# First group of a Mamba-2 layer: the second half of the copies of the turned xs, and their multiplication by the step sizes, stand ahead of the next group's first SiLU step

## The chip, the cores and the metric

The program runs on one NeuronCore of a Trainium2 chip. Four engines compute side by side, each through its own queue in order: TensorE (PE, matrix products; its weight loads are PEld), VectorE (DVE), ScalarE (ACT) and GpSimd (POOL). SyncE (SP) issues most transfers from HBM. An instruction starts when its queue has reached it and the semaphores that it waits for are set. The metric is device time in microseconds (us), lower is better.

## The reference

Two layers on a sequence of 256 tokens with 2048 features: a Mamba-2 (SSD) mixer, then sliding-window attention. The change touches the first. Cut to what matters:

```python
zxbcdt = x @ w_in                                   # z | xs, B, C | dt
xbc = silu(conv4(xbc) + conv_b)                     # causal, depthwise
dt = softplus(dt_raw + dt_bias);  a = -exp(a_log)
x_c = xs * dt[..., None]                            # xs times step sizes
cb = einsum("bcqgn,bcsgn->bgcqs", c_c, b_c)
y_diag = einsum("bgcqs,bgrcqs,bcsgrp->bcqgrp", cb, decay_in, x_c)
y = y_diag + y_off + xs * d_skip
y = y * silu(z);  y = rmsnorm_by_group(y) * norm_w
h = y @ w_out                                       # 8 groups of 8 heads of 64
x = layernorm(alpha * x + h)
```

In the kernel one decay matrix over both chunks of 128 tokens takes the place of the states, so that y is a product of `x_c` with (C B) times decay.

## The kernel before

The projection runs in eight groups of ten blocks: B, C, four blocks of xs, four of z, 128 features each. Block 10*g + b is block b of group g; group 0 takes its blocks in another order (z first, one z last). A block is 48 products of 128x128 by 128x256 on PE (`narrow`, L252): each weight and each x is split into a rounded part and a rest (wh, wl; xH, xL), and three products stand for one. The weights come as two halves of 128x1024 into `wr`; ACT rounds each (wh, L164), DVE subtracts to get the rest (wl, L167). There are four buffers of wh and wl, six halves of wr, and four PSUM buffers `mm`, used in turn by blocks and by output units: a product into a buffer that was used four before waits until DVE has read that one.

After a block of B, C or xs, ACT and DVE make the convolution and SiLU (`conv_silu`): ACT L492, three steps on DVE L494, tanh on ACT L497, one product on DVE L498. z has L582 and L583.

Once the xs of a group are there, `turn_xs` (L604) turns them on DVE in blocks of 32x32 into zx, `carry_xs` (L613) copies them on ACT in 16 pieces (four for each j) into xd, and `scale_xs` (L618) multiplies xd by the step sizes in one DVE operation of 128x1024. Then `ymm` multiplies xd by the decays on PE (L631, "the y products"), DVE multiplies by the rest of the decay and adds the skip term (yz, L636 and L642), `gate` multiplies by z and sums squares on POOL (L647, L649, L653) and splits y for the next product on ACT and DVE (yH L661, yL L662). `norm` sums over features on PE (L671), which needs the last sum of squares from POOL. Output units (`out_unit`, L323 to L325) multiply y by w_out, two PSUM tiles each (token half 0 and 1), and DVE adds each to the residual with the group's scale (L332). The first output unit of group 0 stands behind block 16, the second behind block 17.

The order of the work comes from two places. `plan` holds, for each block number, the steps that are called behind that block's SiLU; `between` holds steps that are called ahead of its SiLU, right after its products. The tile framework then orders the calls on each engine by its own priorities and estimates; operations marked with `keep_in_program_order` stay in the order of the calls. `scale_xs` of group 0 is marked (pinned), the copies are not. In group 0 the y products are planned behind block 13.

The lines that set group 0's steps are

```python
at(xs_at, turn_xs, g)                      # xs_at = 9 in group 0
for n, js in enumerate(((0,), (1,), (2, 3)) if g < 2 else ((0, 1), (2, 3))):
    at(xs_at + n, carry_xs, g, js)         # behind blocks 9, 10, 11
at(xs_at + 2 + (g == 0), scale_xs, g)      # behind block 12 in group 0
at(t + pos["y"], ymm, g)                   # behind block 13 in group 0
```

## Time and profile before

| what | value |
|---|---|
| median of 3 runs | 988.09 us (988.04 to 989.66) |
| the profiled execution's own time | 990.41 us |
| its span, first to last instruction | 988.6 us |
| mean granted TensorE clock over the span | 0.995 of full speed |
| PE busy | 975.7 us, 99% of the span |
| DVE busy | 781.8 us, 79% |
| ACT busy | 662.7 us, 67% |
| POOL busy | 103.8 us, 10% |
| moved by DMA | 198.89 MB, 201 GB/s on average |

Busy times are sums of an engine's instructions. The matrix engine is nearly always busy, so the time is close to its sum of products; what can be won or lost is in the few places in which it stands still or runs at a lower clock. Those are read from the waits of PE, from the timeline of single instructions around them and from the granted clock in short windows. A timeline row gives the start in us, the duration of all of its xN instructions together, engine, line, operation, output<-input, and in brackets how long the engine stood idle before and what it waited for.

### The profile page before, as it was taken

How to read it: one execution, taken by the hardware profiler on the slowest of the kernel's cores; microseconds unless marked ns; L12 is line 12 of the kernel's file. 1: busy time of each engine (PE TensorE's matmuls, PEld its weight loads, DVE VectorE, ACT ScalarE, POOL GpSimd, SP SyncE). 2: the span in 40 equal slices, each digit the busy share in tenths (PEclk: the TensorE clock that was granted, in tenths of full speed). 3: DMA queues.
4: the chain of work that ended last, by engine and by line, in shares of the span. 5: the costliest groups of instructions: out<-in, count | busy, mean ns of one | idle time of the engine just before them, and what ended most of it. 6: DMA issues, size and time to landing. Idle time of an engine off the chain costs nothing.

```text
span 988.6 us, 18074 instructions
## 1 busy us (share of the span) xinstructions
PE 975.7 (99%) x7004; PEld 885.2 (90%) x7004; DVE 781.8 (79%) x1202; ACT 662.7 (67%) x1236; POOL 103.8 (10%) x137
## 2 busy tenths in 40 slices
PE   9997999999999999999999999999999999999998
PEld 8996999999998999999999999888898978978976
DVE  7888797886888696787688687989867678766786
ACT  7596786675677667667667567467367777764772
POOL 0000403004002100300300300402100000000003
PEclk9998999999999999999999999999999999999999
DMA  9698477557657656657665664657654646464542
GB/s 357 241 300 291 139 224 231 191 183 224 204 179 249 209 180 216 204 176 230 189 202 180 204 208 137 206 185 263 229 171 157 196 150 201 152 211 149 192 150 86
DMA packets 61557, 198.89 MB, mean 201 GB/s; under 512 B 6848, under 2 KB 11360, under 8 KB 61216
## 3 DMA queue, kind: packets, MB, share of 16 engines
q1 hardware_dynamic: 58528, 188.53, 58.4%
q0 software_dynamic: 2336, 8.69, 2.7%
q8 instruction: 55, 0.90, 0.4%
q10 hardware_dynamic: 608, 0.52, 0.2%
q14 instruction: 30, 0.25, 0.1%
HBM read 195.49 MB, written 2.23 MB: 200 GB/s over the span
## 4 chain that ended last, share of the span: by engine, by line
PE 93%; ACT 3%; DMA 2%; DVE 1%; issue 1%; DVEq 0%; ACTq 0%
PE mm L252 49%; PE mm L979 11%; PE mm L323 9%; PE mm L324 9%; PE mm L325 9%; PE ax L631 2%; ACT wh L164 1%; DMA rb<-rscr 1%; ACT xd L613 1%; PE ax L1119 1%; ACT e L549 1%; DMA wr<-in_wa 0%; PE ax L1112 0%; DVE wl L167 0%; PE mm L390 0%
## 5 line engine op out<-in xcount | busy, mean ns | idle before, releaser
L167 DVE TENSOR_TENSOR wl<-wr,wh 128x1024 fp32r<-128x1024 f32 (+2 forms) x338 | 392.3, 1179 | 92.3 <-ACT wh L164 90.3
L164 ACT ACTIVATE wh<-wr 128x1024 fp32r<-128x1024 f32 (+2 forms) x338 | 331.9, 1010 | 94.3 <-PE mm L252 34.3
L252 PE MATMUL mm<-xH,wh 128*128 128x256 f32 x1280 | 354.8, 277 | 0.0
L252 PE MATMUL mm<-xH,wl 128*128 128x256 f32 x1280 | 354.0, 277 | 0.1
L252 PE MATMUL mm<-xL,wh 128*128 128x256 f32 x1280 | 354.1, 277 | 0.0
L252 PEld LDWEIGHTS mm<-xH,wh 128*128 128x128 f32 x1280 | 240.6, 188 | 1.7 <-ACT wh L198 0.5
L252 PEld LDWEIGHTS mm<-xL,wh 128*128 128x128 f32 x1280 | 240.6, 188 | 1.3 <-issue 0.3
L252 PEld LDWEIGHTS mm<-xH,wl 128*128 128x128 f32 x1280 | 240.4, 188 | 0.3 <-DVE wl L167 0.3
L323 PE MATMUL mm<-wh,yH 128*128 128x512 f32 x256 | 101.2, 395 | 0.0
L324 PE MATMUL mm<-wh,yL 128*128 128x512 f32 x256 | 99.8, 390 | 0.0
L325 PE MATMUL mm<-wl,yH 128*128 128x512 f32 x256 | 99.7, 389 | 0.0
L647 POOL TENSOR_TENSOR yz<-yz,z 128x256 f32<-128x256 f32 x32 | 33.1, 1044 | 473.7 <-DVE yz L642 444.4
L494 DVE SCALAR_TENSOR_TENSOR cv<-mm,pc,cv 128x255 f32<-128x255 f32 x144 | 68.5, 476 | 5.8 <-ACT cv L492 4.5
L252 PE MATMUL mm<-x1H,wh 128*128 128x256 f32 x256 | 71.9, 281 | 0.0
L252 PE MATMUL mm<-x1L,wh 128*128 128x256 f32 x256 | 71.1, 278 | 0.0
L252 PE MATMUL mm<-x1H,wl 128*128 128x256 f32 x256 | 71.0, 278 | 0.0
L979 PE MATMUL mm<-wh,x1H 128*128 128x512 f32 x160 | 63.1, 394 | 0.0
L979 PE MATMUL mm<-wl,x1H 128*128 128x512 f32 x160 | 61.8, 389 | 0.0
L979 PE MATMUL mm<-wh,x1L 128*128 128x512 f32 x160 | 60.9, 390 | 0.0
L497 ACT ACTIVATE xs<-cv 128x256 f32<-128x256 f32 x32 | 13.3, 416 | 69.7 <-DVE cv L494 69.7
L323 PEld LDWEIGHTS mm<-wh,yH 128*128 128x128 f32 x256 | 48.1, 188 | 10.3 <-DVE z L583 1.0
L325 PEld LDWEIGHTS mm<-wl,yH 128*128 128x128 f32 x256 | 48.1, 188 | 10.2
(228 smaller groups left out, 1459.8 us busy)
## 6 DMA issues: line engine op xcount, KB each, us to landing
wr<-in_wa SPq DMA_DIRECT2D x154, 512.0 KB, 5.2
wr<-in_wo SPq DMA_DIRECT2D x64, 512.0 KB, 4.6
wr<-in_wq SPq DMA_DIRECT2D x32, 512.0 KB, 4.6
wr<-in_wg SPq DMA_DIRECT2D x31, 512.0 KB, 5.2
wr<-in_wb SPq DMA_DIRECT2D x16, 512.0 KB, 4.6
wr<-in_wb SPq DMA_DIRECT2D x32, 256.0 KB, 3.9
rb<-rscr SPq DMA_DIRECT2D x11, 512.0 KB, 4.4
wr<-in_wkv SPq DMA_DIRECT2D x8, 512.0 KB, 5.2
```

Source lines behind the costliest of these rows:

```text
L164: m = nc.scalar.activation(h[:, sl], v, AF.Copy)
L167: m = nc.vector.tensor_tensor(l[:, sl], v, h[:, sl].bitcast(F32), ALU.subtract)
L252: m = nc.tensor.matmul(ps, a, b, start=first and i == 0, stop=last and i == 2)
L323: pinned(nc.tensor.matmul(ps, aH[:, k, hs], u.h[:, ks], start=k == 0 and add is None, stop=False), pin)
L324: pinned(nc.tensor.matmul(ps, aL[:, k, hs], u.h[:, ks], start=False, stop=False), pin)
L325: pinned(nc.tensor.matmul(ps, aH[:, k, hs], u.l[:, ks], start=False, stop=k == 3), pin)
L494: nc.vector.scalar_tensor_tensor(a[:, sft:], ps[:, : S - sft], w(3 - sft), a[:, sft:], ALU.mult, ALU.add)
L497: nc.scalar.activation(dst, a[:], AF.Tanh)
L549: m = nc.scalar.activation(e[:, h, cols], rb[:, h, c * P :], AF.Relu, scale=-1.0, bias=rtk[:, c, h0 + h : h0 + h + 1])
L631: nc.tensor.matmul(ps[64 * r : 64 * r + 64, cols], st.xd[:, c, i, 64 * r : 64 * r + 64], e[:, 256:] if c else e[:, :256], start=c == 0, st ...
L647: nc.gpsimd.tensor_tensor(v, v, st.z[i][:], ALU.mult)
L979: m = nc.tensor.matmul(ps[:], (x1H, x1L, x1H)[i][:, kk, hs], (u.h, u.h, u.l)[i][:, ks], start=(kk, i) == (0, 0), stop=ui == 3 and (k, i) = ...
```

## The change

```diff
-        for n, js in enumerate(((0,), (1,), (2, 3)) if g < 2 else ((0, 1), (2, 3))):
-            at(xs_at + n, carry_xs, g, js)
-        at(xs_at + 2 + (g == 0), scale_xs, g)
+        if g == 0:
+            at(9, carry_xs, 0, (0,))
+            between[10] = [(carry_xs, 0, (1,))]
+            between[11] = [(carry_xs, 0, (2, 3)), (scale_xs, 0)]
+        else:
+            for n, js in enumerate(((0,), (1,), (2, 3)) if g < 2 else ((0, 1), (2, 3))):
+                at(xs_at + n, carry_xs, g, js)
+            at(xs_at + 2, scale_xs, g)
```

The copies of j = 1 are called ahead of block 10's SiLU, those of j = 2 and 3 and the multiplication ahead of block 11's. The other groups are as before. On ACT the 16 copies keep their places. On DVE the multiplication moves. In the rows below xd_1023 is the tile of the turned xs of group 0, cv a SiLU's convolution sums (cv_1088 in one, cv_1092 in the other, of block 10), and wl_1180 or wl_1181 the rests of block 14's weights.

DVE, around the SiLU of block 10, before:

```order
L494 TENSOR_SCALAR cv_1088<-mm_1038,pc,cv_1088 128x253
L167 TENSOR_TENSOR wl_1180<-wr_1181,wh_1179 128x1024
L498 TENSOR_SCALAR bt_1087<-bt_1087,cv_1088 128x256
L167 TENSOR_TENSOR wl_1180<-wr_1183,wh_1179 128x1024
L167 TENSOR_TENSOR wl_1249<-wr_1250,wh_1248 128x1024
```

and now:

```order
L494 TENSOR_SCALAR cv_1092<-mm_1038,pc,cv_1092 128x253
L618 TENSOR_TENSOR xd_1023<-xd_1023,dtx 128x1024
L498 TENSOR_SCALAR bt_1091<-bt_1091,cv_1092 128x256
L167 TENSOR_TENSOR wl_1181<-wr_1182,wh_1180 128x1024
L167 TENSOR_TENSOR wl_1181<-wr_1184,wh_1180 128x1024
L167 TENSOR_TENSOR wl_1249<-wr_1250,wh_1248 128x1024
```

The multiplication (L618) has come in right behind block 10's third convolution step, ahead of both halves of wl for block 14. Its old place was 15 operations further on.

PE, at the y products of group 0 (ax_1317 and ax_1329), before (mm_1382 is block 14):

```order
L252 MATMUL mm_1382<-xH,wl_1180 128x256
L252 MATMUL mm_1382<-xH,wh_1179 128x256
L631 MATMUL ax_1317<-e_726,xd_1023 64x256 x2
L631 MATMUL ax_1317<-e_726,xd_1023 64x128 x2
```

and now (mm_1258 is block 13):

```order
L252 MATMUL mm_1258<-xL,wh_1104 128x256
L252 MATMUL mm_1258<-xH,wl_1105 128x256
L631 MATMUL ax_1317<-e_726,xd_1023 64x256 x2
L631 MATMUL ax_1317<-e_726,xd_1023 64x128 x2
```

The y products stood behind the first ten products of block 14 and now stand ahead of all 48 of them, right behind block 13.

DVE, behind the SiLU of block 12, before (wl_1446: the rests for the first output unit; cv_1308: block 13; yz, yH, yL: group 0's y):

```order
L618 TENSOR_TENSOR xd_1023<-xd_1023,dtx 128x1024
L167 TENSOR_TENSOR wl_1446<-wr_1447,wh_1445 128x1024
L494 TENSOR_SCALAR cv_1308<-mm_1258,pc,cv_1308 128x255
L167 TENSOR_TENSOR wl_1446<-wr_1449,wh_1445 128x1024
L494 TENSOR_SCALAR cv_1308<-mm_1258,pc,cv_1308 128x254
L636 TENSOR_TENSOR yz_1316<-ax_1317,el_942 128x512
L494 TENSOR_SCALAR cv_1308<-mm_1258,pc,cv_1308 128x253
```

and now, a little further on in the same stretch:

```order
L642 TENSOR_SCALAR yz_1316<-xs_790,pc,yz_1316 128x256
L636 TENSOR_TENSOR yz_1316<-ax_1329,el_942 128x512
L498 TENSOR_SCALAR xs_1307<-xs_1307,cv_1308 128x256
L642 TENSOR_SCALAR yz_1316<-xs_861,pc,yz_1316 128x256
L642 TENSOR_SCALAR yz_1316<-xs_934,pc,yz_1316 128x256
L662 TENSOR_SCALAR yL_1350<-yz_1316,pc,yH_1349 128x256
L167 TENSOR_TENSOR wl_1446<-wr_1449,wh_1445 128x1024
L662 TENSOR_SCALAR yL_1350<-yz_1316,pc,yH_1349 128x256 x3
```

The second half of wl_1446 has gone from between the convolution steps of block 13 to behind the first yL. ACT and POOL each have one swap of neighbours there (the first yH ahead of a tanh, a transfer issued ahead of an addition).

## The prediction

> **What bounds the kernel now.** I read the page first, then what PE waited for.

> ```profile
> span 988.6 us, 18074 instructions
> PE 975.7 (99%) x7004; PEld 885.2 (90%) x7004; DVE 781.8 (79%) x1202; ACT 662.7 (67%) x1236; POOL 103.8 (10%) x137
> PE 93%; ACT 3%; DMA 2%; DVE 1%; issue 1%; DVEq 0%; ACTq 0%
> ...
> PE ax L631 <- DVE xd L618: 7.1, 1, 7.1
> PE ax L372 <- DVE zero L360: 1.0, 1, 1.0
> ```

> PE is busy for 99% of the span and makes up 93% of the chain that ended last. It waits for another engine twice: 1.0 us at the start, and once for 7.1 us, at the y products (L631), for the multiplication that the change moves. So I read the timeline around that wait, engine by engine, and then the pieces of the chain there and at the same steps later.

> ```profile
> 79.26 2.06 ACT L613 COPY xd<-zx 32x256 f32<-32x256 f32 x5
> 79.27 1.52 DVE L494 SCALAR_TENSOR_TENSOR cv<-mm,pc,cv 128x255 f32<-128x255 f32 x3 [0.43 <-ACT cv L492]
> 82.44 1.22 DVE L167 TENSOR_TENSOR wl<-wr,wh 128x1024 fp32r<-128x1024 f32 x1 [1.66 <-ACT wh L164]
> 87.56 0.28 PE L252 MATMUL mm<-xH,wh 128*128 128x256 f32 x1
> 88.61 0.28 PE L252 MATMUL mm<-xH,wh 128*128 128x256 f32 x1
> 94.40 0.42 DVE L498 SCALAR_TENSOR_TENSOR xs<-xs,cv 128x256 f32<-128x256 f32 x1 [0.54 <-ACT xs L497]
> 94.74 1.22 DVE L618 TENSOR_TENSOR xd<-xd,dtx 128x1024 f32<-128x1024 f32 x1
> ```

> ```profile
> 96.02 5.39 PE ax L631 x32
> 101.41 15.40 PE mm L252 x134
> 123.36 5.47 PE mm L252 x48
> 150.67 2.75 PE ax L631 x32
> ```

> The last copy into xd ends at 79.26 + 2.06 = 81.3. The multiplication runs at 94.74, 13 us later, though it needs nothing else: it stood in its place in DVE's queue. PE ended its ten early products of block 14 (87.56 to 88.61, the first and the last of them) at 88.9 and stood until 96.0. Group 1's y products take 2.75, these took 5.39. The clock says why:

> ```profile
> 88.00:89.00 1.00, 0.89 (x8) 0.69 (x6) 0.68 (x2) 0.19 (x1) 0.00 (x0) 1.00 0.68 254
> 91.00:92.00 1.00, 0.00 (x0) 0.00 (x0) 1.00 (x3) 0.56 (x1) 0.00 (x0) 0.56 0.88 311
> 96.00:97.00 1.00, 0.98 (x6) 0.61 (x8) 1.00 (x1) 0.71 (x1) 0.00 (x0) 0.50 0.77 315
> 101.00:102.00 1.00, 1.00 (x9) 0.67 (x7) 0.67 (x2) 1.00 (x3) 0.92 (x2) 0.82 0.77 307
> ```

> The granted clock is the third number from the end. It is 0.56 in 91 to 92, so it fell to one half at about 91.1 (0.12 of that us at full speed), 2.2 us after PE stopped. It is 0.82 in 101 to 102, so it came back at about 101.4, 5.3 us after PE resumed.

> **The change, part by part.** *The multiplication on DVE.* In its new place DVE has finished the convolution steps at 80.8, the copies end at 81.3, and DVE stood idle for 1.66 us ahead of 82.44. It runs there, 81.3 to 82.5, and the y products have xd 5 us before PE asks. Cost: the two wl halves of block 14 behind it end about 0.4 later; block 14 is then used behind the y products only, so they are covered by 2.75. What follows on DVE until 94.4 is about 0.3 late.

> *The wait of PE.* Block 13 ends at 87.56. The y products follow at once, with a warm clock: 87.6 to 90.35. Blocks 14 to 16 of 5.47 each end at 106.8. In before, they end at 101.41 + 15.40 = 116.8 less a few hundredths. PE is ahead by 7.1 (the wait) + 2.64 (5.39 less 2.75) = 9.8 us. That much would be the gain if all else came early too. It doesn't: DVE, ACT and POOL did other work during the wait and are not 9.8 us ahead. These rows tell what is late next.

> ```profile
> 99.92 0.87 DVE L642 SCALAR_TENSOR_TENSOR yz<-xs,pc,yz 128x256 f32<-128x256 f32 x2
> 100.53 1.18 POOL L647 TENSOR_TENSOR yz<-yz,z 128x256 f32<-128x256 f32 x1 [29.34 <-ACT xs L497]
> 102.61 0.96 DVE L642 SCALAR_TENSOR_TENSOR yz<-xs,pc,yz 128x256 f32<-128x256 f32 x1
> 106.57 0.48 DVE L494 SCALAR_TENSOR_TENSOR cv<-mm,pc,cv 128x255 f32<-128x255 f32 x1 [1.37 <-ACT cv L492]
> 106.97 3.50 DVE L662 SCALAR_TENSOR_TENSOR yL<-yz,pc,yH 128x256 fp32r<-128x256 f32 x2
> 109.43 0.74 POOL L653 TENSOR_TENSOR sq<-sq,sq 128x256 f32<-128x256 f32 x1
> 110.79 1.21 DVE L167 TENSOR_TENSOR wl<-wr,wh 128x1024 fp32r<-128x1024 f32 x1
> 116.00 1.52 DVE L494 SCALAR_TENSOR_TENSOR cv<-mm,pc,cv 128x255 f32<-128x255 f32 x3 [2.14 <-ACT cv L492]
> 116.65 0.50 PE L671 MATMUL ax<-cc,sq 128*128 128x1 f32 x4
> 117.67 0.48 PE L323 MATMUL mm<-wh,yH 128*128 128x512 f32 x1
> 127.88 1.37 DVE L332 SCALAR_TENSOR_TENSOR xr<-mm,r,xr 128x512 f32<-128x512 f32 x2
> 128.67 0.39 PE L323 MATMUL mm<-wh,yH 128*128 128x512 f32 x1
> 131.40 0.39 PE L323 MATMUL mm<-wh,yH 128*128 128x512 f32 x1
> ```

> *First new wait, at norm (L671).* It needs POOL's last sum, which ended at 110.2 for a PE that came at 116.65. POOL starts when DVE has made the first yz (99.92 plus one of two operations). DVE reaches that at 98.0: gone from ahead of it are the multiplication (1.2), the second half of wl_1446 (1.1) and a convolution step (0.4), and 0.8 is paid that the next paragraph names. So POOL starts at 98.6 and, with its 9.6 us (100.53 to 110.17), ends at 108.2. PE comes at 106.8: a wait of about 1.5. Behind it are queued the C B product and the first output unit, 109.3 (1.0 after norm, as 117.67 to 116.65).

> *Second and third, for PSUM.* Block 17 writes the buffer of block 15, free when DVE's three steps at 116.00 end (117.5); the second unit's second half (131.40) writes the buffer of the first unit's first half, free when the first of the two additions at 127.88 ends (128.6). In before, that leaves 2.8 us to spare. So the gain that lasts is 2.8 plus what DVE's additions come earlier. From the wl at 110.79 to 127.88 DVE and ACT do the same work in both kernels and wait for PE nowhere, so the question is what the stretch from 94.40 to 110.79 loses. It loses the multiplication (1.2) and the wait for block 14 (1.4, since the block now ends at 95.8). It pays the 0.3 from above and about 0.5 for waiting on ACT's conversion, which the multiplication had hidden, as here at a like place:

> ```profile
> 90.20 1.22 DVE L167 TENSOR_TENSOR wl<-wr,wh 128x1024 fp32r<-128x1024 f32 x1 [0.52 <-ACT wh L164]
> 159.87 1.76 DVE L167 TENSOR_TENSOR wl<-wr,wh 128x1024 fp32r<-128x1024 f32 x1
> ```

> That is 1.8 us earlier. But the second half of wl_1446 and a SiLU product have moved to where POOL is at work, and there DVE is slower: a yz took 0.96 instead of 0.43, a wl 1.76 instead of 1.21, and two yL 3.50. Bounds for the shift: 2.6 earlier (nothing paid) and nothing. I take 1.1, nearer to the slowed rows (1.8 less 0.55 and 0.53 is 0.7), because POOL works through the whole stretch. So the addition ends at 127.5, block 15's buffer is free at 116.4.

> PE then: first unit 109.3, block 17 at 115.0 (5.69 on, as 117.67 to 123.36), waits 1.4 to 116.4, second unit at 121.7, its second half at 124.5, waits 3.0 to 127.5. Gain there 131.4 - 127.5 = 3.9, and 9.8 less 1.5, 1.4 and 3.0 is 3.9 too. Behind that PE is again what all others wait for: the wl of block 18 follows the additions directly on DVE and PE needs it 2.7 later; the gain stays to the end.

> [...]

> *The clock.* A wait of 3.0 is longer than the 2.2 after which the clock fell. No row shows its price at this length: nothing if it holds, 2.64 as in the wait of 7.1. The ends are far apart; the wait is past the point at which the clock fell, so it is nearer to the row of 2.64 than to nothing: I take 1.4. If it falls at norm instead, most of that is taken out of the waits behind. Gain 3.9 - 1.4 = 2.5.

> *DMA and queues.* SP's order is unchanged. One issue waits for the second half of wl_1446, which now ends about 6 us later (near 105 instead of 98.6):

> ```profile
> 97.12 1.85 SPq L155 DMA_DIRECT2D wr<-in_wa  x2
> wr<-in_wa SPq DMA_DIRECT2D x154, 512.0 KB, 5.2
> 124.80 2.95 ACT L164 ACTIVATE wh<-wr 128x1024 fp32r<-128x1024 f32 x3
> ```

> It lands near 111 and ACT reads it at about 124: cover of 13 us, cost nothing. POOL's transfer, one place earlier, is read 40 us later.

> The sum: a span of 988.6 - 2.5 = 986.1; the profiled execution 990.41 - 2.5 = 987.9. That execution is 2.3 above the median of the runs shown, so against the median: 988.09 - 2.5 = **985.6**.

> **The rivals.** *The clock holds* in the third wait: 988.09 - 3.9 = 984.2. For it: the wait is less than half of 7.1. Against it: the fall after 2.2. [...]

> *DVE and POOL exclude each other in full.* POOL's 9.6 less its two issues of about 0.7 is 8.3; DVE has eight operations of 0.42 and a wl of 1.21 there, 4.6. One after another from 98.6 they end at 111.5, and with two convolution steps of 0.4 the wl at 110.79 comes at 112.3, 1.5 late. So do the additions: gain 2.8 - 1.5 = 1.3, less up to 1.4 for the clock: 986.8 to 988.2. For it: the 3.50 of two yL. Against it: the 0.87 of two yz beside POOL's start.

> *Slower.* The same collisions, worse: each of these nine operations takes the 1.75 of the yL at 106.97. From 98.9 that is 15.8; with 0.6 for the yz read from PSUM and 0.8 for two convolution steps the wl comes at 116.1. The additions are 5.3 late, PE's second half 2.5 later than before: 990.6. It decides from 2.8 on, where the spare time is used up. Against it: POOL's work ends long before.

> *Nothing comes back:* 988.09 - 9.8 = 978.3; against it the L653 and L332 rows. *It doesn't do what it says*, PE waiting for something else at L631: 988.1; against it, the wait names L618 alone and group 1's y products wait for nothing.

> **How the numbers follow.** A measurement of this kernel can tell about 0.2%, 2.0 us, from no change. Forecast 985.6: 0.45, its own range 984.7 (clock price 0.5) to 987.0 (shift 0.5, price 1.9). Clock holds, 983.4 to 984.7: 0.25. Full exclusion: 0.15. Nothing comes back: 0.03. No effect: 0.04. Slower: 0.08. Faster by over 2.0, below 986.1: 0.36 of the forecast's, 0.25, 0.03 and 0.01 of exclusion: 0.65. Slower 0.09, the rest same, 0.26. The range 983.3 to 988.0 reaches over the first three and leaves out what lies beyond.

> **What would show it.** L618 at about 81.3 and no wait of L631 for it; the y products 2.75 long near 87.6; a wait of L671 on POOL of 1 to 3 us; waits of L252 and L323 on DVE L494 and L332; a clock under 1.0 near 127 to 132. Wrong: a gain above 6 (no waits), a wait of L631 that stays, or wl of blocks 14 to 18 late.

## The result, and the profile after

The changed kernel takes 985.32 us in the median of eight runs (984.70 to 986.33). The kernel before, in eight runs (the three of the table above among them), takes 988.84 us (986.81 to 991.18). The ratio is 0.9965, with a 95% interval of 0.9954 to 0.9977: faster by 0.35%, about 3.5 us. The forecast was 985.6 from a base of 988.09, that is a gain of 2.5, and the range 983.3 to 988.0 holds the time. The profiled execution has a span of 984.1 us, 4.5 less than before, at a mean granted clock of 0.999.

The page of the changed kernel and its list of what PE waited for (total us, times, longest) answer to the first lines of the prediction:

```profile
PE 973.6 (99%) x7004; PEld 883.8 (90%) x7004; DVE 783.3 (80%) x1202; ACT 662.7 (67%) x1236; POOL 103.2 (10%) x137
...
PE ax L671 <- POOL sq L653: 2.6, 1, 2.6
PE mm L323 <- DVE xr L332: 2.4, 1, 2.4
PE ax L372 <- DVE zero L360: 1.0, 1, 1.0
```

The wait of 7.1 us is gone. Two new ones stand in its place: 2.6 us at the norm, and 2.4 us at the second half of the second output unit. The timeline around them, in the order of time:

```profile
78.73 2.06 ACT L613 COPY xd<-zx 32x256 f32<-32x256 f32 x5
78.74 1.52 DVE L494 SCALAR_TENSOR_TENSOR cv<-mm,pc,cv 128x255 f32<-128x255 f32 x3 [0.44 <-ACT cv L492]
80.83 1.23 DVE L618 TENSOR_TENSOR xd<-xd,dtx 128x1024 f32<-128x1024 f32 x1 [0.57 <-ACT xd L613]
...
87.20 2.82 PE L631 MATMUL ax<-e,xd 128*64 128x256 f32 x32
98.26 0.73 POOL L647 TENSOR_TENSOR yz<-yz,z 128x256 f32<-128x256 f32 x1 [27.61 <-DVE yz L642]
100.65 2.92 DVE L642 SCALAR_TENSOR_TENSOR yz<-xs,pc,yz 128x256 f32<-128x256 f32 x2
103.89 1.75 DVE L167 TENSOR_TENSOR wl<-wr,wh 128x1024 fp32r<-128x1024 f32 x1
104.53 2.34 POOL L649 TENSOR_TENSOR sq<-yz 128x256 f32<-128x256 f32 x2
105.57 2.45 DVE L662 SCALAR_TENSOR_TENSOR yL<-yz,pc,yH 128x256 fp32r<-128x256 f32 x3
107.94 0.99 DVE L494 SCALAR_TENSOR_TENSOR cv<-mm,pc,cv 128x255 f32<-128x255 f32 x2
108.34 0.74 POOL L653 TENSOR_TENSOR sq<-sq,sq 128x256 f32<-128x256 f32 x1
109.13 0.61 PE L671 MATMUL ax<-cc,sq 128*128 128x1 f32 x4 [2.56 <-POOL sq L653]
...
126.06 1.36 DVE L332 SCALAR_TENSOR_TENSOR xr<-mm,r,xr 128x512 f32<-128x512 f32 x2
126.82 0.50 PE L323 MATMUL mm<-wh,yH 128*128 128x512 f32 x1 [2.37 <-DVE xr L332]
```

The multiplication (L618) runs at 80.83 in DVE's idle time, the y products take 2.82 near 87.2, and POOL's last sum ends at 109.08 for a PE that had come at 106.57. The second half of the output unit starts at 126.82, for 131.40 before. Behind it both kernels need the same time: 988.6 - 131.40 = 857.2 and 984.1 - 126.82 = 857.3. So the whole difference between the traces was made by the time at which that row starts.

Not all of it comes from the change. DVE's row at block 10 (the second above), which no moved operation precedes, is at 79.27 before and at 78.74 here, and lies between 76.74 and 78.82 in the experiments. Most of these differences arise far ahead of the operations that were edited: one and the same subtraction on DVE (wl, L167) starts at 51.07 to 53.07 in the ten traces, behind a wait of ACT of 2.6 to 4.9 us for a transfer (rb). What sets that wait was not tested. PE moves less: its y products start between 86.92 and 87.72 wherever they wait for nothing. Below, a DVE time is therefore given as its distance from that row. The additions (L332) are 127.88 - 79.27 = 48.61 behind it before and 126.06 - 78.74 = 47.32 now, 1.3 earlier. Of the 4.6 us at the second half, 0.5 is where that row lies and 4.05 is left.

The chain of work that ended last shows what holds the first group now (start, us, engine and line):

```profile
80.82 1.06 ACT wh L164
...
100.73 2.84 DVE yz L642 x2
...
123.41 0.69 DVE e L597
...
125.04 1.08 DVE zx L604 x3
126.13 0.65 DVE xr L332
```

Before, the chain came through the multiplication to the y products and stayed on PE. Now it stays on DVE and ACT until 126.8. In this execution the granted clock (third number from the end) did not fall in either wait:

```profile
108.00:109.00 1.00, 0.00 (x0) 0.00 (x0) 0.96 (x4) 0.00 (x0) 0.99 (x2) 1.00 0.53 213
...
125.00:126.00 1.00, 0.00 (x0) 0.00 (x0) 1.00 (x4) 0.92 (x1) 0.00 (x0) 1.00 0.66 262
```

### The profile page after: what moved, and what is told of

It reads as the page before. It is cut to its first block, busy times and chain, and to the rows that moved or that the text cites. A ratio compares the mean times of both kernels' runs of the same rounds, so it can differ in the third digit from the quotient of the medians.

```text
span 984.1 us, 18075 instructions
## 1 busy us (share of the span) xinstructions
PE 973.6 (99%) x7004; PEld 883.8 (90%) x7004; DVE 783.3 (80%) x1202; ACT 662.7 (67%) x1236; POOL 103.2 (10%) x137
## 4 chain that ended last, share of the span: by engine, by line
PE 86%; DVE 5%; ACT 4%; DMA 3%; issue 1%; SPq 1%; ACTq 0%; DVEq 0%
PE mm L252 43%; PE mm L984 11%; PE mm L323 9%; PE mm L325 9%; PE mm L324 9%; PE ax L631 2%; DVE wl L167 2%; DMA wr<-in_wa 1%; ACT wh L164 1%; ACT e L549 1%; DMA rb<-rscr 1%; DMA xr<-in_first 1%; ACT xd L613 1%; PE ax L1124 1%; SPq L192 1%
## 5 line engine op out<-in xcount | busy, mean ns | idle before, releaser
L167 DVE TENSOR_TENSOR wl<-wr,wh 128x1024 fp32r<-128x1024 f32 (+2 forms) x338 | 392.8, 1181 | 88.5 <-ACT wh L164 86.6
L164 ACT ACTIVATE wh<-wr 128x1024 fp32r<-128x1024 f32 (+2 forms) x338 | 332.1, 1010 | 92.4 <-PE mm L252 32.7
L252 PE MATMUL mm<-xH,wh 128*128 128x256 f32 x1280 | 355.0, 277 | 0.0
L252 PE MATMUL mm<-xL,wh 128*128 128x256 f32 x1280 | 354.2, 277 | 0.0
L252 PE MATMUL mm<-xH,wl 128*128 128x256 f32 x1280 | 354.0, 277 | 0.0
L252 PEld LDWEIGHTS mm<-xH,wh 128*128 128x128 f32 x1280 | 240.8, 188 | 2.0 <-ACT wh L198 0.3
L252 PEld LDWEIGHTS mm<-xL,wh 128*128 128x128 f32 x1280 | 240.6, 188 | 0.9
L252 PEld LDWEIGHTS mm<-xH,wl 128*128 128x128 f32 x1280 | 240.6, 188 | 0.0
L323 PE MATMUL mm<-wh,yH 128*128 128x512 f32 x256 | 101.3, 396 | 2.4 <-DVE xr L332 2.4
L647 POOL TENSOR_TENSOR yz<-yz,z 128x256 f32<-128x256 f32 x32 | 32.7, 1030 | 469.6 <-DVE yz L642 469.6
L494 DVE SCALAR_TENSOR_TENSOR cv<-mm,pc,cv 128x255 f32<-128x255 f32 x144 | 68.4, 476 | 4.5 <-ACT cv L492 3.1
L252 PE MATMUL mm<-x1H,wh 128*128 128x256 f32 x256 | 71.9, 281 | 0.0
L252 PE MATMUL mm<-x1L,wh 128*128 128x256 f32 x256 | 71.1, 278 | 0.0
L252 PE MATMUL mm<-x1H,wl 128*128 128x256 f32 x256 | 71.1, 278 | 0.0
L323 PEld LDWEIGHTS mm<-wh,yH 128*128 128x128 f32 x256 | 48.1, 188 | 13.0 <-DVE xr L332 2.8
L497 ACT ACTIVATE xs<-cv 128x256 f32<-128x256 f32 x32 | 13.3, 415 | 66.8 <-DVE cv L494 66.8
L325 PEld LDWEIGHTS mm<-wl,yH 128*128 128x128 f32 x256 | 48.1, 188 | 10.2
## 6 DMA issues: line engine op xcount, KB each, us to landing
wr<-in_wa SPq DMA_DIRECT2D x154, 512.0 KB, 5.2
wr<-in_wo SPq DMA_DIRECT2D x64, 512.0 KB, 4.4
wr<-in_wq SPq DMA_DIRECT2D x32, 512.0 KB, 4.5
wr<-in_wg SPq DMA_DIRECT2D x31, 512.0 KB, 5.0
wr<-in_wb SPq DMA_DIRECT2D x16, 512.0 KB, 4.3
rb<-rscr SPq DMA_DIRECT2D x11, 512.0 KB, 4.1
wr<-in_wkv SPq DMA_DIRECT2D x8, 512.0 KB, 4.8
```

Of the source, the lines that this page charges most:

```text
L164: m = nc.scalar.activation(h[:, sl], v, AF.Copy)
L167: m = nc.vector.tensor_tensor(l[:, sl], v, h[:, sl].bitcast(F32), ALU.subtract)
L252: m = nc.tensor.matmul(ps, a, b, start=first and i == 0, stop=last and i == 2)
L323: pinned(nc.tensor.matmul(ps, aH[:, k, hs], u.h[:, ks], start=k == 0 and add is None, stop=False), pin)
L325: pinned(nc.tensor.matmul(ps, aH[:, k, hs], u.l[:, ks], start=False, stop=k == 3), pin)
L494: nc.vector.scalar_tensor_tensor(a[:, sft:], ps[:, : S - sft], w(3 - sft), a[:, sft:], ALU.mult, ALU.add)
```

## The experiments

All start from the changed kernel. The theory: early waits of PE are forgotten, since the second half of the output unit hangs on DVE's additions, and a wait that leaves the granted clock as it is costs only its length. Its rivals stand with each experiment.

**The copies early, the multiplication later.** The multiplication goes behind block 11's SiLU; the copies are called as in the changed kernel.

```diff
-            between[11] = [(carry_xs, 0, (2, 3)), (scale_xs, 0)]
+            between[11] = [(carry_xs, 0, (2, 3))]
+            at(11, scale_xs, 0)
```

> The multiplication stands behind the SiLU of block 11, between its old and its new place; all else is the changed kernel. Theory (the time is set by VectorE's chain of additions, and PE's early waits are given back later): the multiplication ends near 90, PE waits for it about 3 us at the y products, and then the waits at norm (2.6) and at the second output unit (2.4) shrink by about as much in all; the second half of the second output unit starts within 0.8 us of the changed kernel's 126.8, and the time is that of the changed kernel within 1 us (ratio to the kernel before 0.9965 to 0.9975). Rival (each us that PE waits at the y products costs a us): about 3 us slower than the changed kernel, a ratio of 0.999 to 1.000.

Measured: 986.45 us, ratio 0.9963 (0.9950 to 0.9977) to the kernel before, span 982.8 in the profiled execution. Its waits and rows:

```profile
PE mm L323 <- DVE xr L332: 2.5, 1, 2.5
PE ax L631 <- DVE xd L618: 1.7, 1, 1.7
...
77.04 1.52 DVE L494 SCALAR_TENSOR_TENSOR cv<-mm,pc,cv 128x255 f32<-128x255 f32 x3 [0.44 <-ACT cv L492]
87.38 1.22 DVE L618 TENSOR_TENSOR xd<-xd,dtx 128x1024 f32<-128x1024 f32 x1
...
124.64 1.37 DVE L332 SCALAR_TENSOR_TENSOR xr<-mm,r,xr 128x512 f32<-128x512 f32 x2
```

PE waits 1.7 us for the multiplication again, and the wait at the norm has gone. The 1.7 is less than the 3 expected because block 10's row lies 1.7 earlier here than in the changed kernel. The additions stand 124.64 - 77.04 = 47.60 behind that row, for 47.32, and the second half 48.4, for 48.1. By the ratio the time is that of the full change, 0.9963 for 0.9965; the traced execution is the fastest of the ten, and the nine others lie at 985.93 to 987.12 with mean clocks of 0.996 to 0.998. So the early wait costs nothing that shows, as the theory says, and a part of the move is enough for the gain: against block 10's row the multiplication stands 15.5 us on before, 10.3 here and 2.1 in the changed kernel, and the last 8 bring nothing by themselves.

**POOL later.** Three writes of zeros ahead of the last square of group 0, some 0.31 us each.

```diff
         q = ap.tile([P, S], F32, tag="sm", name=nm("sq"), bufs=NSM)
+        for _ in range(3 if (g, i) == (0, 3) else 0):
+            nc.gpsimd.memset(q[:], 0.0)
         nc.gpsimd.tensor_tensor(q[:], v, v, ALU.mult)
```

> Three writes of a constant of 128x256 on POOL ahead of the last square of group 0, which overwrites them. Theory: they take 0.3 us each, norm's wait on POOL grows from 2.6 to about 3.5, the wait at the second output unit shrinks from 2.4 to about 1.5, and the time is that of the changed kernel within 0.5 us (ratio 0.9965). Rival (the wait at norm is on the path): 0.9 us slower, the wait at the second output unit still 2.4. [...]

Measured: 986.46 us (984.38 to 990.08), ratio 0.9962 (0.9941 to 0.9983); span 985.0. This interval of 2 us to either side holds the theory and its rival, 0.9 us apart, so the time alone does not decide. L655 and L673 are L653 and L671 of the kernel before, two lines on:

```profile
PE ax L673 <- POOL sq L655: 2.8, 1, 2.8
...
77.95 1.52 DVE L494 SCALAR_TENSOR_TENSOR cv<-mm,pc,cv 128x255 f32<-128x255 f32 x3 [0.45 <-ACT cv L492]
125.09 1.37 DVE L332 SCALAR_TENSOR_TENSOR xr<-mm,r,xr 128x512 f32<-128x512 f32 x2
...
109.00:110.00 1.00, 0.14 (x1) 0.15 (x1) 1.00 (x3) 0.01 (x1) 0.80 (x1) 0.70 0.12 41
...
116.00:117.00 1.00, 1.00 (x5) 0.86 (x4) 0.00 (x0) 1.00 (x2) 0.00 (x0) 0.89 0.35 143
```

The wait at the norm grew to 2.8 only, not to 3.5. Here the clock fell, in a wait only 0.2 longer than that of the changed kernel: down from 109.4 to 116.2, 6.8 us. PE came to the second half 17.9 us after the norm instead of 15.3, so the slow clock cost it 2.6. No wait for the additions is left. They stand 47.14 behind block 10's row, 125.09 after 77.95, so the writes on POOL did not move them; but PE started the second half at 127.73, 1.9 after the first of them had ended. So of a price paid early the later wait takes in no more than its own length, and what goes beyond is lost. The other runs agree: the three with a mean clock of 1.000 took 984.38 to 984.72, the seven with 0.995 to 0.998 took 984.81 to 990.08. So the loss goes with the clock; that it fell at the norm in the runs that were not traced is argued.

**The additions later.** `turn_xs` of group 1, which DVE does just ahead of the additions, is done twice, and in a second kernel three times (a 3 in the place of the 2); the extra turns write the same values again.

```diff
-        for i in range(4):
+        for i in list(range(4)) * (2 if g == 1 else 1):
```

> The four transposes of group 1's xs are done twice on VectorE, which puts four operations of 0.36 us ahead of the two additions. Theory: the second half of the second output unit starts 1.4 us later than in the changed kernel, its wait grows from 2.4 to 3.8, and the span grows by 1.4 if the clock holds, by 2.4 to 4 if it falls. Rival (the addition is not what PE waits for, or there is slack left): no change.

> The same with the transposes done three times: eight operations more. Theory: 2.9 us later, a wait of 5.2 to 5.3, and the clock falls in it, since it fell in the wait of 7.1 us of the kernel before 2.2 us after PE had stopped: half speed from then until 3 to 5 us after PE resumes, so the span grows by 2.9 plus 1 to 2.6. Rival: the clock holds for any wait below 7, and the span grows by 2.9.

Measured, one run each: 987.22 and 988.82 us beside a kernel before of 990.13, spans 985.4 and 987.0. Twice:

```profile
PE ax L671 <- POOL sq L653: 2.7, 1, 2.7
PE mm L323 <- DVE xr L332: 2.3, 1, 2.3
...
78.72 1.52 DVE L494 SCALAR_TENSOR_TENSOR cv<-mm,pc,cv 128x255 f32<-128x255 f32 x3 [0.44 <-ACT cv L492]
127.33 1.37 DVE L332 SCALAR_TENSOR_TENSOR xr<-mm,r,xr 128x512 f32<-128x512 f32 x2
...
109.00:110.00 1.00, 0.90 (x6) 0.87 (x7) 1.00 (x1) 0.00 (x0) 0.05 (x1) 0.97 0.84 213
...
113.00:114.00 1.00, 1.00 (x5) 0.76 (x5) 0.00 (x0) 1.00 (x3) 0.05 (x1) 0.82 0.63 164
```

and three times:

```profile
PE mm L323 <- DVE xr L332: 5.2, 1, 5.2
PE ax L671 <- POOL sq L653: 0.9, 1, 0.9
...
76.78 1.52 DVE L494 SCALAR_TENSOR_TENSOR cv<-mm,pc,cv 128x255 f32<-128x255 f32 x3 [0.44 <-ACT cv L492]
126.75 1.36 DVE L332 SCALAR_TENSOR_TENSOR xr<-mm,r,xr 128x512 f32<-128x512 f32 x2
...
125.00:126.00 1.00, 0.00 (x0) 0.00 (x0) 1.00 (x4) 0.00 (x0) 0.00 (x0) 0.77 0.00 0
...
132.00:133.00 1.00, 1.00 (x7) 0.87 (x6) 1.00 (x2) 1.00 (x2) 0.00 (x0) 0.82 1.04 348
```

Each set of four extra turns puts the additions 1.3 or 1.4 us further behind block 10's row: 48.61 and 49.97, for 47.32. So the end does hang on DVE's order. Done twice, the clock fell for 3.4 us right behind the wait at the norm and PE came later by itself, so the wait at the additions did not grow. Done three times, it fell in the wait at the additions, 3.2 us after PE stopped at 122.3, for 6.8 us; behind the second half this execution needs 987.0 - 127.51 = 859.5 us, for 857.3: there the slow clock costs 2.2, and nothing behind takes it back. The span grew by 2.9, the very number of the rival in which the clock holds, but that is chance: block 10's row lay 2.0 earlier than in the changed kernel, and against it the second half came 2.65 later, to which the 2.2 is added.

**The changed kernel again.**

> The changed kernel once more, on the same chip as the next three, for a comparison between them. Both theories: 985.3 us, ratio 0.9965 to the kernel before. What is open is only its clock: the theory that drops come on a grid of 3.41 us that runs free of the program says that in another execution a wait of 2.4 to 2.6 at the norm (L671) or at L323 may fall differently on that grid, so a profile may show one drop of one or two times 3.41 us, with an end up to 2 us later; the theory that a wait under some fixed length never drops the clock says 1.00 throughout again.

Measured: 985.92 us, ratio 0.9959 (0.9944 to 0.9974), and a span of 984.1 again. The waits are 2.3 at the norm and 2.5 at the additions, and the clock held in both. The 3.41 us fit the falls seen by then, of 10.24 us in the kernel before and of 6.82, 3.42 and 6.82 in the last three runs; that they come on a grid was the author's supposition. This run is the base of the next three, which ran on the same chip.

**C times B behind the additions.** Group 1's first multiplication of e by C times B (L597), 1.7 us on DVE, is planned one block later.

```diff
-            by = (16, 17)
+            by = (17, 17)
```

> Group 1's multiplication of e by C times B (L597, first head pair) stands one block later, and so behind the two additions (L332) on DVE instead of ahead of them. Theory (the third wait is the DVE's work ahead of the additions, and nothing else): the additions start about 1.7 us earlier against block 10's row, 47.32 down to about 45.6, the wait of L323 goes from 2.4 to about 0.7, and the time from 985.3 to about 983.6. Rival A (the wait only moves: what was late becomes a wait at block 17 or where the C times B product is read): L323's wait shrinks, another of 1 to 2 us appears within ten us, and the time stays at 985.3. Rival B (the additions are held by something else than DVE's order, the matrix product itself): the wait stays 2.4.

Measured: 985.17 us, ratio 0.9948 (0.9932 to 0.9964), 0.75 below the base, a difference that the intervals do not tell from none. The profiled execution:

```profile
PE ax L671 <- POOL sq L653: 2.5, 1, 2.5
...
PE mm L325 <- DVE wl L167: 0.4, 1, 0.4
...
78.82 1.52 DVE L494 SCALAR_TENSOR_TENSOR cv<-mm,pc,cv 128x255 f32<-128x255 f32 x3 [0.44 <-ACT cv L492]
109.00:110.00 1.00, 0.78 (x5) 0.78 (x6) 1.00 (x2) 0.00 (x0) 0.16 (x1) 0.80 0.68 205
...
124.47 0.71 DVE L332 SCALAR_TENSOR_TENSOR xr<-mm,r,xr 128x512 f32<-128x512 f32 x1
```

The additions come 45.65 behind block 10's row, 1.67 earlier, as the theory said, and the wait for them is gone. But in this execution the clock fell right behind the wait at the norm, from 109.6 to 113.0, and PE came 1.2 us later by itself; a wait of 0.4 on a wl follows. So most of the 1.7 is not in its span (983.9). The fastest two of the six runs took 983.45 and 983.87, the four others 984.84 to 985.97. The theory's mechanism is shown; its time of 983.6 is not the median. The clock goes with the difference between those runs: the mean clock is 1.000 in the fastest two and 0.998 or 0.999 in the four others. That it fell at the norm in all of these is argued, since one of them was traced.

**The squares on ACT.** Group 0's four squares go from POOL to ACT.

```diff
-        nc.gpsimd.tensor_tensor(q[:], v, v, ALU.mult)
+        if g == 0:
+            nc.scalar.activation(q[:], v, AF.Square)
+        else:
+            nc.gpsimd.tensor_tensor(q[:], v, v, ALU.mult)
```

> Group 0's four squares are made by ACT instead of POOL; the product with z stays on POOL. Theory (the norm's wait is POOL's stretched chain, and what is saved there is given back at the second half of the output unit, which hangs on DVE alone): the norm's wait of 2.6 falls under 1, the wait of L323 grows by as much, 2.4 to about 4, and the time stays within 0.5 of 985.3. Rival (DVE and POOL slow one another, so DVE with fewer POOL operations beside it reaches the additions earlier): the additions come 0.5 to 1 us earlier against block 10's row, 47.3 to about 46.5, and the time falls by as much, to about 984.5. ACT's evictions (L492, L613) later by 0.3 to 0.6 a square would show as a wait at block 16 or 17 and cost up to 1 us.

Measured: 982.48 us (982.20 to 985.65), ratio 0.9932 (0.9916 to 0.9949), 3.4 below the base. The rows below keep their line numbers:

```profile
PE mm L323 <- DVE xr L332: 1.1, 1, 1.1
...
76.96 1.52 DVE L494 SCALAR_TENSOR_TENSOR cv<-mm,pc,cv 128x255 f32<-128x255 f32 x3 [0.43 <-ACT cv L492]
98.54 0.87 DVE L642 SCALAR_TENSOR_TENSOR yz<-xs,pc,yz 128x256 f32<-128x256 f32 x2
104.54 0.99 DVE L494 SCALAR_TENSOR_TENSOR cv<-mm,pc,cv 128x255 f32<-128x255 f32 x2
122.00 1.37 DVE L332 SCALAR_TENSOR_TENSOR xr<-mm,r,xr 128x512 f32<-128x512 f32 x2
```

The theory fell here, and its rival won by more than it had said. The two yz that took 2.92 take 0.87; block 15's steps (107.94 in the changed kernel, 104.54 here) come 1.6 us earlier against block 10's row; and the additions stand 45.04 behind it, 2.3 earlier. So the squares on POOL had slowed DVE, whose operations stand in the same order in both kernels there; how the 1.6 at block 15 become 2.3 at the additions, on the way over ACT's and DVE's steps for blocks 15 and 16, was not taken apart. At the norm PE no longer waits, and at the additions it waits 1.1. In this execution block 10's row lies 1.78 earlier than in the changed kernel's; with the row at its place there, the wait would be 2.9 and the gain at the second half 126.82 - 122.76 - 1.78 = 2.3. The medians are 3.4 apart, but with six and five runs that spread over 3.5 and 1.5 us the two numbers do not contradict each other.

**Both.** C times B behind, and the squares on ACT.

> Both edits of the last two runs in one kernel. Theory (two waits of one chain, each with its own cause, and the later one sets the end): with the additions about 1.7 us earlier and the norm no longer late, neither wait is left above 1 us; about 982 us, and the gain over the changed kernel is more than that of either edit alone. Rival (DVE's order alone sets the end): the same time as with C times B behind alone, about 983.6. Rival (a new wait, at block 17's PSUM tile or at the next group's SiLU): no better than 985.

Measured: 981.52 us (981.03 to 983.46), ratio 0.9919 (0.9903 to 0.9935), 4.4 below the changed kernel beside it and the fastest kernel here, as the theory said. Span 978.9, and PE waits for another engine only at the program's start:

```profile
PE ax L372 <- DVE zero L360: 1.0, 1, 1.0
...
76.74 1.52 DVE L494 SCALAR_TENSOR_TENSOR cv<-mm,pc,cv 128x255 f32<-128x255 f32 x3 [0.44 <-ACT cv L492]
120.10 1.37 DVE L332 SCALAR_TENSOR_TENSOR xr<-mm,r,xr 128x512 f32<-128x512 f32 x2
```

The additions stand 43.36 behind block 10's row: 3.96 earlier than in the changed kernel, which is the sum of the 1.67 and 2.28 of the two edits alone. Of the 9.8 us by which the change puts PE ahead, both edits together keep nearly all: the span is 988.6 - 978.9 = 9.7 shorter than before. In the median it is less, 8.0 by the ratio: the traced execution of the kernel before lies above its median.

## Why the prediction was right, point by point

- **The multiplication, and the wait of 7.1.** Right: L618 at 80.83 (said 81.3), the y products at a clock of 1.00, 2.82 long, near 87.2, no wait there.
- **The wait at the norm.** Right in kind, too small: 2.6 for 1.5. POOL's chain from the first yz lasted 98.26 to 109.08, 10.8 us instead of the 9.6 taken from before; its own operations vary too: two squares took 2.34 from 104.53, beside DVE's wl and yL, and the one at 99.07 took 0.68.
- **The wait at block 17's buffer.** It did not come. The 1.4 said for it went into the larger wait at the norm: the buffer was free at 115.69, and PE came to block 17 at 115.84.
- **The wait at the additions.** Right in place, 2.4 for 3.0. Together the three waits were 5.0, for 5.9.
- **DVE's shift and the lasting gain.** Right: the additions came 1.3 earlier (said 1.1), and 4.05 of the gain is left at the second half (said 3.9). That the early waits do not matter was shown by the copies early, the multiplication later; that DVE's order does, by the additions later and by C times B behind.
- **The clock.** This is the term that was mis-sized: "I take 1.4" for the third wait, measured nothing in two traces of the changed kernel. The rival "The clock holds" names what happened in these two. In other runs the clock seems to have fallen without a price that shows (last section), as a side remark of the prediction had it: a fall at the norm is mostly taken out of the waits behind. The gain without a clock price, 3.9, is nearer to the measured 3.5 (0.35% of 988.84; 2.3 to 4.5 by the interval) than the 2.5 forecast. That the predicted time, 985.6 for 985.3, came out nearer than its gain is luck: the base of three runs, 988.09, lay 0.75 below the median of all eight. The price itself is not nothing: at this place it was 2.2 when the wait was 5.2. What failed is the reading of one row, "2.2 us after PE stopped", as a length after which the clock falls (below).
- **The rival of full exclusion** is out: it put the additions 1.5 later, they came 1.3 earlier. That POOL slows DVE is shown by the squares on ACT: two yz in 2.92 beside POOL's squares, 0.87 without them. That the two exclude each other in full was the author's supposition, and no run shows it: the sum that puts every operation of both in a row through the whole stretch does not come out.
- **The transfers** cost nothing that shows: PE waits for no transfer in the first group (its three waits, of 2.6, 2.4 and 1.0 us, are for engines).

## What to carry to other kernels

When a long wait of the busiest engine is removed, look for the last place at which that engine still meets the slower ones: the gain is what they come earlier there plus the spare time they had, and the waits in between only divide up the rest. Read that place's own chain for what holds it; here two operations that stood in DVE's way, one of its own and one of a neighbour that slowed it, were worth about as much as the change itself: 4.4 us beside 989.9 - 985.92 = 4.0 on the same chip. Compare moments between two traces by their distance from a row that the change can't reach, since DVE lay up to 2.5 us apart at that row.

## What the runs showed of the hardware

What starts the steps was not shown. The end of PE's work does not: the falls come 2.2 to 3.5 us after it. Nor does the start of the span: they come at 91.12, 109.40, 109.60, 109.94 and 125.54 us, which leave 2.5, 0.3, 0.5, 0.8 and 2.8 over whole steps of 3.41. So whether the clock falls for a wait of 2.5 us may depend on how the wait lies on these steps; that is the author's inference, and no run shows a grid: each of these traces has only one fall and one return there. Nor need PE stand for a whole step ahead of a fall: before, PE worked until 88.9, and the clock fell at 91.1, so that the last 3.4 us ahead of the fall, from 87.7, were busy for a third (1.19 of 3.41).

One fall of 3.4 us at the norm made PE 1.2 to 1.4 us later (16.5 and 16.7 us from the norm to the second half, for 15.3), and the kernel not by that much, as long as a wait stood behind it. The mean clock over the span tells how often it fell: the traces without a fall in this stretch have 0.999 or 1.000, those with one step 0.997 or 0.998, with two 0.996, and the kernel before, with three, 0.995. By this scale, which is an inference, it fell in eight of the thirteen runs of the changed kernel. The five with 0.999 have spans of 982.9 to 984.1, the six with 0.998 spans of 983.1 to 984.5, and the two with less 984.3 and 984.8. One step thus costs this kernel nothing that shows.
